# A hybrid decoder trunk on one core: who makes the low halves of four weight tiles of layer 0

## The chip, the cores and the metric

One of the eight cores of a Trainium2 chip runs the whole program. The metric is device time in microseconds (us) of one execution. The core has TensorE (PE in the profile, PEld for its weight loads), VectorE (DVE), ScalarE (ACT), GpSimd (POOL) and SyncE (SP); each runs its own instructions in order, and semaphores hold one back for another. TensorE multiplies into eight banks of PSUM; everything else lies in SBUF. Transfers (DMA) are issued by SP, by ScalarE and by GpSimd; only those of GpSimd add what they bring to what lies in SBUF.

## The reference, cut to what matters

Two layers of this, on 512 tokens of 1024 features, in float32:

```
h = rmsnorm(x) * (1 + sc1) + sh1                       # adaLN from c
u = h @ w_in                                           # 1024 x (256 + 3*256 + 3*512 + 3*1024)
u_pool, u_conv, b_conv, c_conv, q, k, v, gates = split(u)
y_pool = pool_mixer(u_pool)                            # trailing windows 2, 4, 8, 16
y_conv = b_conv * causal_short_conv(c_conv * u_conv)   # width 3
y_attn = moba_attention(rope(rmsnorm(q)), rope(rmsnorm(k)), v)   # blocks of 256
x += g1 * (sum_i sigmoid(gate_i) * (y_i @ p_i)) @ w_out
h2 = rmsnorm(x) * (1 + sc2) + sh2
x += g2 * ((silu(h2 @ w_gate) * (h2 @ w_up)) @ w_down)
```

The change touches four tiles of `w_in` in the first layer: the two that hold the lower half of the keys' rows, and the two column blocks (4 and 5) of `b_conv`, which gate the convolution.

## The kernel before, in words

**Layout.** Activations lie transposed, features on the 128 partitions and 512 tokens along the row. Weights come from HBM in one stream that the host has laid out in the order of use, as tiles of up to eight blocks of 128 by 128 (512 KB).

**Three products for one.** TensorE multiplies in a rounded form of float32 (`fp32r`). To keep float32's accuracy each operand is split into a high half, its rounded value, and a low half, what the rounding left. `mm3` adds three products, high by high, high by low and low by high. So each weight tile is fetched into a `raw` tile, its high half is copied into a `whi` tile by ScalarE, and its low half is made in a `wlo` tile, in one of two ways:

- `split_w` (lines 397 to 404): ScalarE copies the high half (line 399), VectorE subtracts it from the raw tile (line 402). Both read the raw tile.
- `split_by_transfer` (lines 416 to 424): ScalarE copies the high half (line 419) and then the negated high half into the `wlo` tile (line 421); then GpSimd issues a transfer that fetches the weights a second time and adds them to it (line 423). Only the first copy reads the raw tile.

There are three `raw` tiles and five each of `whi` and `wlo`. A `raw` tile is fetched anew by SP (line 239) when its last reader is through; a `whi` or `wlo` tile is written anew when TensorE has used it.

**Order.** The list `items` holds all weight tiles in the order of use. `load_w` loads the next one, `next_w` hands one out and keeps up to four loaded ahead. TensorE's instructions, and VectorE's that are marked with `pin`, keep the program's order; for the rest (ScalarE's copies, transfers) a planner sets the order on each engine at build time by its own estimate of when each can run. On the chip each engine then goes through its list in that order. Which buffer of a ring a tile gets follows from that order too.

**The stretch around the change, layer 0.** First come the queries and three column blocks (lines 987 to 1015), then three column tiles (6, 3 and 7). Then the keys and values, by `keys_values` (line 1043) with tiles from the class `KeyValue` (line 296): seven products of half-size matrices in place of eight, called forms, of 24 matmuls of 512 columns each, in the order B21, B11, R1, -V, B22, T3, T4. Each form uses two tiles, of 12 matmuls each. The first two forms (numbers 0 and 1 in `load`, line 322) take the keys' weights as they are, the others take sums that GpSimd's transfers build in two `w` tiles (`summed`, lines 313 to 315) and `big` tiles (`summed_rows`, lines 350 to 354). In layer 0 the first two forms are split by transfer, in layer 1 by VectorE (line 335). The raw tiles of the second form stay for VectorE's additions at line 338.

Behind the forms come single columns of eight blocks (`feature_tile`, 24 matmuls): gate columns 20, 28 and 21, then columns 4 and 5, each followed by a product of the pool mixer, then gate column 29 and the rest of the gates. `by_transfer` (line 426) decides which of them are split by transfer: those of the pool and attention projections and the columns above 20, so 28, 21 and 29 but not 20, 4 and 5. Meanwhile attention's pieces for the heads are dealt out among the matmuls. VectorE's last instruction of a piece of attention, line 872, hands its output to ScalarE and to TensorE's next matmuls.

Of the kernel before, what the change touches and what calls it, by code (L numbers as in the profile page):

```python
# [25 lines left out]
KT = D // P  # L26
# [15 lines left out]
C_BLOCKS = 8  # L42
# [41 lines left out]
def hybrid_trunk(ctx, tc, xT, ws, ada, cols, pool_w, qk_w, crow, pos, con, out):  # L84
# [12 lines left out]
    def nm(s):  # L97
        uid[0] += 1
        return f"{s}{uid[0]}"

    def bigt(dt=F32R):
        return big.tile([P, S], dt, tag="big", name=nm("big"))
# [10 lines left out]
    def w4(shape, dt=F32):  # L113
        return work.tile(shape, dt, tag="w4", name=nm("w4"), bufs=6)
# [42 lines left out]
    def pin(ins):  # L157
        return tc.keep_in_program_order(ins)
# [66 lines left out]
    def runs(l, blocks):  # L225

        i = 0
        while i < len(blocks):
            off, n, at = place[blocks[i]]
            j = i + 1  # L230
            while j < len(blocks) and place[blocks[j]] == (off, n, at + j - i):
                j += 1
            src = ws[l, off:off + n * P * P].rearrange("(p f) -> p f", p=P)
            yield i, j - i, src[:, at * P:(at + j - i) * P]
            i = j

    def fetch(tile, l, blocks):
        for i, n, src in runs(l, blocks):
            nc.sync.dma_start(tile[:, i:i + n].rearrange("p b n -> p (b n)"), src)
# [37 lines left out]
    class GateUp:  # L277
# [9 lines left out]
        def load(self, sub):  # L287
            if sub < 2:
                return self.pair[sub].first()
            if sub < 6:  # L290
                return self.pair[sub % 2].sums(sub // 2 - 1)
            raw = rawt()
            fetch(raw, self.l, self.pair[0].blocks(1, 1) + self.pair[1].blocks(1, 1))
            return split_w(raw, C_BLOCKS)

    class KeyValue:
# [25 lines left out]
        def load(self, sub):  # L322
            form, cp = divmod(sub, 2)
            if sub == 0:
                self.near, self.far = [None] * 2, [None] * 2
            if sub == 2:
                self.x = [w4([P, C_BLOCKS, P]) for _ in range(2)]
                for i in range(2):
                    self.summed(self.x[i], (1, 1), i)
            if form < 2:  # L330
                kk = 1 - form
                raw = self.raw(kk, 0, cp)
                if form == 1:
                    self.near[cp] = raw
                return split_by_transfer(raw, self.l, self.blocks(kk, 0, cp)) if self.l == 0 else split_w(raw, C_BLOCKS)
            if form in (2, 3):
                w = split_w(self.x[cp], C_BLOCKS)
                pin(V.tensor_add(self.x[cp], self.x[cp], self.near[cp]))
                if form == 2:
                    self.near[cp] = self.raw(1, 0, cp)  # L340
                    self.far[cp] = [bigt(F32) for _ in range(2)]
                    self.summed_rows(self.far[cp], (0, 0), cp)
                return w
            if form == 4:
                return split_w(self.x[cp], C_BLOCKS)
            if form == 5:
                return split_rows(self.far[cp])
            return split_w(self.raw(1, 1, cp), C_BLOCKS)
# [26 lines left out]
    for l in range(L):  # L375
# [7 lines left out]
        for blocks in first_part + list(feed_forward()):  # L383
            if not isinstance(blocks, list):
                if isinstance(blocks, int):
                    blocks = GateUp(l, blocks)
# [7 lines left out]
    def rawt():  # L394
        return wp.tile([P, C_BLOCKS, P], F32, tag="raw", name=nm("raw"), bufs=RAW)

    def split_w(raw, n):
        hi = wp.tile([P, C_BLOCKS, P], F32R, tag="whi", name=nm("whi"), bufs=5)
        A.activation(hi[:, :n], raw[:, :n], AF.Copy)  # L399
        lo = wp.tile([P, C_BLOCKS, P], F32R, tag="wlo", name=nm("wlo"), bufs=5)  # L400
        with tc.issue_after(hold[0].ins) if hold[0] is not None else nullcontext():
            ins = V.tensor_sub(lo[:, :n], raw[:, :n], f32(hi)[:, :n])  # L402
        pin(ins)
        return hi, lo


    def split_rows(tiles):
        hi = wp.tile([P, C_BLOCKS, P], F32R, tag="whi", name=nm("whi"), bufs=5)
        lo = wp.tile([P, C_BLOCKS, P], F32R, tag="wlo", name=nm("wlo"), bufs=5)
        rows = lambda t, i: t[:, 4 * i:4 * i + 4].rearrange("p b n -> p (b n)")  # L410
        for i, tile in enumerate(tiles):
            A.activation(rows(hi, i), tile, AF.Copy)
            pin(V.tensor_sub(rows(lo, i), tile, f32(rows(hi, i))))
        return hi, lo

    def split_by_transfer(raw, l, blocks):
        n = len(blocks)
        hi = wp.tile([P, C_BLOCKS, P], F32R, tag="whi", name=nm("whi"), bufs=5)
        A.activation(hi[:, :n], raw[:, :n], AF.Copy)  # L419
        lo = wp.tile([P, C_BLOCKS, P], F32R, tag="wlo", name=nm("wlo"), bufs=5)  # L420
        A.activation(lo[:, :n], f32(hi)[:, :n], AF.Copy, scale=-1.0)  # L421
        for i, m, src in runs(l, blocks):
            nc.gpsimd.dma_start(lo[:, i:i + m].rearrange("p b n -> p (b n)"), src, accum_op=ALU.add)  # L423
        return hi, lo

    def by_transfer(blocks):
        return blocks[0][0] in ("pool", "attn") or blocks[0][0] == "in" and blocks[0][2] > 20 and len(blocks) == KT

    split_after, last_hi = [None], [None]
# [3 lines left out]
    def load_w():  # L433
        while at[1] < min(at[0] + 1 + SUMS_AHEAD, len(items)):
            sums, sub = items[at[1]]
            if sums is not None and sub == 0:
                sums.begin()
            at[1] += 1
        sums, what = items[at[0]]
        at[0] += 1  # L440
        if sums is not None:
            return sums.load(what)
        l, blocks = what
        raw = rawt()
        with tc.issue_after(fetch_after[0].ins) if fetch_after[0] is not None else nullcontext():
            fetch(raw, l, blocks)
        if by_transfer(blocks):
            return split_by_transfer(raw, l, blocks)
        with tc.issue_after(split_after[0].ins) if split_after[0] is not None else nullcontext():
            return split_w(raw, len(blocks))  # L450
# [3 lines left out]
    def next_w(ahead=None):  # L454
        ahead = ahead_now[0] if ahead is None else ahead
        while at[0] < len(items) and len(loaded) <= ahead:
            loaded.append(load_w())
        return loaded.popleft()
# [97 lines left out]
    def ada_tasks(l, parts, early=False):  # L556
        every = [(part, j) for part in parts for j in range(KT)]
        kept, out = [], []
        load = lambda n: ada_load(l, *every[n], early, kept)

        def step(n):
            if early and n + 1 < len(every):
                load(n + 1)
            if not early:
                load(n)
            ada_step(l, *every[n], kept)

        if early:
            out.append((1.2, lambda: load(0)))
        for n, (part, j) in enumerate(every):  # L570
            out.append((1.2, lambda n=n: step(n)))
            if j == KT - 1:
                out.append((0.2, lambda part=part: ada_end(l, part)))
        return out
# [133 lines left out]
    def second(nrm, l, i, bank):  # L708

        hold[0] = None  # L710
        nrm.stat(BLOCK, S, bank)
        for k, lo, hi in HALVES[3:]:
            nrm.apply(l, i, k, lo, hi)

        loaded.append(load_w())
        for k, lo, hi in REST:
            nrm.apply(l, i, k, lo, hi)
# [240 lines left out]
    norm.first_hi(0)  # L958
    fetch_after[0] = step[4]
    loaded.append(load_w())  # L960
    split_after[0] = last_hi[0]
    norm.first_lo(0)
# [651 lines left out]
```

## Time and profile before

| | |
|---|---|
| median of 3 runs | 1435.55 us (1434.87 to 1435.87) |
| the profiled execution | 1438.11 us |
| its span, first to last instruction | 1436.3 us |
| granted clock of TensorE over the span | 0.998 |
| weight tiles split by transfer (line 423) | 66, 861 ns to issue one |
| weight tiles split by VectorE (line 402), fetched or summed | 170 and 84, 1181 and 1220 ns each |
| transfers of GpSimd (queue 0) | 80.76 MB, 27.8% of 16 engines' span |
| transfers of SP (queue 1) | 177.37 MB, 35.5% of 16 engines' span |

How to read it. The span is cut into what each engine does. A row of a timeline gives the start and the duration in us, engine, line, operation, what it writes and reads, and in brackets how long the engine was idle before and who ended that. A row of the waits gives the engine, what waited, who ended the wait, and then the total in us, the number of times and the longest. The chain is the work that ended last, followed back from the end: each piece is what the next one waited for. All times are in us from the start of the span. `whi` and `wlo` are the high and low halves of weights, `big` those of activations, `mm` and `pair` banks of PSUM; matmuls into `mm` with `wlo` second (`mm<-big,wlo`) are columns, those into `pair` with `wlo` first are forms.

### The profile page before, as it was taken

Reading aid. Unit: us, or ns where it says so; the run is one execution under the profiler, and the core shown is the slowest. Engines: PE = TensorE matmul, PEld = TensorE weight load, DVE = VectorE, ACT = ScalarE, POOL = GpSimd, SP = SyncE. Lnnn points to the kernel's source line nnn. Section 1 sums busy time; section 2 is a strip of 40 time slices with the busy share of each in tenths; the row PEclk is TensorE's granted clock in tenths of the full one; section 3 lists DMA queues with packets and bytes.
Section 4 is the critical chain, followed back from the end, with each engine's and each line's share of the span. In section 5 each row is a group of like instructions: output and inputs, shape, how many; then the busy total and the mean of one; then the engine's idle time right before and its main releaser. Section 6 shows DMA issues by size and latency. Waiting matters only on the chain.

```text
span 1436.3 us, 22185 instructions
## 1 busy us (share of the span) xinstructions
PE 1425.6 (99%) x8308; PEld 1256.1 (87%) x8308; DVE 1045.0 (73%) x1978; ACT 765.1 (53%) x1275; POOL 179.5 (12%) x246
## 2 busy tenths in 40 slices
PE   9999999999999999999999999999999999999999
PEld 8877887887989998989998888888889989999997
DVE  7889767649886867667788986665778747657663
ACT  5767667743554452535455676667336525425450
POOL 0111101110200210211001111111020103111200
PEclk9999999999999999999999999999999999999999
DMA  9878668897636766746527676667872537636522
GB/s 349 232 200 213 149 168 199 199 320 243 172 122 212 205 177 205 191 125 212 199 78 248 171 196 141 159 158 187 300 213 85 138 109 186 175 107 179 138 86 85
DMA packets 96587, 259.67 MB, mean 181 GB/s; under 512 B 12248, under 2 KB 24928, under 8 KB 96480
## 3 DMA queue, kind: packets, MB, share of 16 engines
q1 hardware_dynamic: 67312, 177.37, 35.5%
q0 software_dynamic: 28576, 80.76, 27.8%
q8 instruction: 65, 1.06, 0.3%
q14 instruction: 42, 0.34, 0.1%
q10 hardware_dynamic: 592, 0.14, 0.0%
HBM read 256.12 MB, written 2.10 MB: 180 GB/s over the span
## 4 chain that ended last, share of the span: by engine, by line
PE 89%; DVE 4%; DMA 4%; ACT 2%; issue 1%; SPq 0%; DVEq 0%; ACTq 0%; POOLq 0%
PE mm L155 77%; PE pair L155 11%; DMA raw<-in_ws 2%; PE mm L161 2%; DMA wlo<-in_ws 1%; DVE w L479 1%; DVE wlo L402 1%; DMA x<-in_xT 0%; DVE tmp L683 0%; DVE big L690 0%; ACT whi L419 0%; ACT wlo L421 0%; DVE big L702 0%; DVE big L1252 0%; ACT big L701 0%
## 5 line engine op out<-in xcount | busy, mean ns | idle before, releaser
L155 PE MATMUL mm<-big,whi 128*128 128x512 f32 (+1 forms) x4334 | 1073.4, 339 | 0.8 <-ACT big L701 0.6
L155 PEld LDWEIGHTS mm<-big,whi 128*128 128x128 f32 x4334 | 741.3, 190 | 87.2 <-issue 2.2
L155 PE MATMUL mm<-big,wlo 128*128 128x512 f32 (+1 forms) x2167 | 732.1, 338 | 1.1 <-DMA wlo<-in_ws 1.1
L155 PEld LDWEIGHTS mm<-big,wlo 128*128 128x128 f32 x2167 | 411.0, 190 | 46.0 <-ACT whi L419 1.5
L399 ACT ACTIVATE whi<-raw 128x1024 fp32r<-128x1024 f32 (+2 forms) x170 | 174.3, 1028 | 159.1 <-PE mm L155 92.5
L402 DVE TENSOR_TENSOR wlo<-raw,whi 128x1024 fp32r<-128x1024 f32 (+2 forms) x170 | 199.2, 1181 | 41.7 <-ACT whi L399 41.2
L399 ACT ACTIVATE whi<-w 128x1024 fp32r<-128x1024 f32 x84 | 88.8, 1058 | 154.6 <-PE mm L155 87.1
L402 DVE TENSOR_TENSOR wlo<-w,whi 128x1024 fp32r<-128x1024 f32 x84 | 101.1, 1220 | 29.1 <-ACT whi L399 28.4
L479 DVE SCALAR_TENSOR_TENSOR w<-w,csil 128x1024 f32<-128x1024 f32 x88 | 105.1, 1219 | 13.2 <-DMA w<-in_ada 13.2
L1301 DVE SCALAR_TENSOR_TENSOR x<-mm,mod,x 128x512 f32<-128x512 f32 (+1 forms) x89 | 61.5, 693 | 70.2 <-PE mm L155 69.9
L423 POOL DMA_DIRECT2D wlo<-in_ws x66 | 56.9, 861 | 401.4 <-ACT wlo L421 321.7
L261 POOL DMA_DIRECT2D w<-in_ws x72 | 47.1, 666 | 453.6 <-DVE wlo L402 210.9
L419 ACT ACTIVATE whi<-raw 128x1024 fp32r<-128x1024 f32 x66 | 70.0, 1061 | 50.8 <-PE mm L155 29.5
L155 PE MATMUL pair<-whi,big 128*128 128x512 f32 x256 | 83.0, 389 | 0.0
L263 POOL DMA_DIRECT2D w<-in_ws x72 | 64.4, 915 | 138.0 <-DMA w<-in_ws 131.8
L155 PE MATMUL pair<-big,whi 128*128 128x256 f32 (+1 forms) x392 | 78.9, 298 | 0.0
L421 ACT ACTIVATE wlo<-whi 128x1024 fp32r<-128x1024 f32 x66 | 69.3, 1054 | 0.6
L155 PEld LDWEIGHTS pair<-big,whi 128*128 128x128 f32 x392 | 63.4, 191 | 2.8
L155 PE MATMUL pair<-big,wlo 128*128 128x256 f32 (+1 forms) x196 | 58.4, 298 | 0.0
L155 PEld LDWEIGHTS pair<-whi,big 128*128 128x128 f32 x256 | 48.1, 188 | 9.9
L701 ACT ACTIVATE big<-big 128x512 fp32r<-128x512 f32 x52 | 32.4, 626 | 38.6 <-DVE big L1294 18.2
L155 PE MATMUL pair<-wlo,big 128*128 128x512 f32 x128 | 50.0, 390 | 1.4 <-DMA wlo<-in_ws 1.4
(239 smaller groups left out, 1411.7 us busy)
## 6 DMA issues: line engine op xcount, KB each, us to landing
raw<-in_ws SPq DMA_DIRECT2D x146, 512.0 KB, 4.3
w<-in_ada SPq DMA_DIRECT2D x88, 512.0 KB, 5.7
w<-in_ws POOLq DMA_DIRECT2D x144, 256.0 KB, 4.5
wlo<-in_ws POOLq DMA_DIRECT2D x66, 512.0 KB, 6.5
raw<-in_ws SPq DMA_DIRECT2D x64, 256.0 KB, 3.8
raw<-in_ws SPq DMA_DIRECT2D x24, 384.0 KB, 3.5
raw<-in_ws SPq DMA_DIRECT2D x16, 448.0 KB, 5.3
raw<-in_ws SPq DMA_DIRECT2D x36, 128.0 KB, 2.9
```

What stands on the lines that cost most here:

```text
L155: tc.keep_in_program_order(T.matmul(*a, **k))
L161: tc.keep_in_program_order(T.transpose(*a))
L261: nc.gpsimd.dma_start(dst, self.source(0, 1))
L263: nc.gpsimd.dma_start(dst, self.source(*other), accum_op=ALU.add)
L399: A.activation(hi[:, :n], raw[:, :n], AF.Copy)
L402: ins = V.tensor_sub(lo[:, :n], raw[:, :n], f32(hi)[:, :n])
L419: A.activation(hi[:, :n], raw[:, :n], AF.Copy)
L421: A.activation(lo[:, :n], f32(hi)[:, :n], AF.Copy, scale=-1.0)
L423: nc.gpsimd.dma_start(lo[:, i:i + m].rearrange("p b n -> p (b n)"), src, accum_op=ALU.add)
L479: return V.scalar_tensor_tensor(aw, aw, 1.0, csil, op0=ALU.mult, op1=ALU.mult, accum_out=mod[l][:, part, j:j + 1])
L701: A.activation(hi, src, AF.Copy)
L1301: V.scalar_tensor_tensor(x[k][:, lo:hi], src, mod[l][:, part, k:k + 1], x[k][:, lo:hi], op0=ALU.mult, op1=ALU.add)
```

## The change

In layer 0 the first form of keys and values (number 0, B21) makes its two low halves with VectorE, as layer 1 does, and columns 4 and 5 make theirs with ScalarE's negating copy and an adding transfer. Layer 1 and all other tiles are as before. `by_transfer` gets the layer as an argument.

```diff
@@ -332,7 +332,7 @@
                 raw = self.raw(kk, 0, cp)
                 if form == 1:
                     self.near[cp] = raw
-                return split_by_transfer(raw, self.l, self.blocks(kk, 0, cp)) if self.l == 0 else split_w(raw, C_BLOCKS)
+                return split_by_transfer(raw, self.l, self.blocks(kk, 0, cp)) if self.l == 0 and form else split_w(raw, C_BLOCKS)
             if form in (2, 3):
@@ -423,7 +423,9 @@
-    def by_transfer(blocks):
+    def by_transfer(blocks, l):
+        if l == 0 and len(blocks) == KT and blocks[0] in (("in", 0, 4), ("in", 0, 5)):
+            return True
         return blocks[0][0] in ("pool", "attn") or blocks[0][0] == "in" and blocks[0][2] > 20 and len(blocks) == KT
@@ -444,7 +446,7 @@
-        if by_transfer(blocks):
+        if by_transfer(blocks, l):
             return split_by_transfer(raw, l, blocks)
```

## The prediction, made before the changed kernel was run

> **What bounds the kernel now.** I read the page's first part, then TensorE's waits over the whole run, then the chain that ended last around the stretch that the change touches. The page:
>
> ```profile
> span 1436.3 us, 22185 instructions
> ...
> PE 1425.6 (99%) x8308; PEld 1256.1 (87%) x8308; DVE 1045.0 (73%) x1978; ACT 765.1 (53%) x1275; POOL 179.5 (12%) x246
> ```
>
> TensorE (PE) is busy for 99% of the span; 1436.3 - 1425.6 = 10.7 us is all that it idles. The change adds and removes no matmul, so it can gain only from those 10.7 us. TensorE's waits, from the longest on:
>
> ```profile
> PE pair L155 <- DMA wlo<-in_ws: 1.4, 1, 1.4
> PE mm L155 <- DVE tmp L872: 1.4, 1, 1.4
> ...
> PE mm L155 <- DMA wlo<-in_ws: 1.1, 1, 1.1
> ```
>
> Two of them wait for a low half (wlo) that a transfer adds to. Where they lie, from the chain of 50 to 125 us, and from TensorE's timeline, with the first low half of column 4 in a fence of its own, for later:
>
> ```profile
> 68.34 11.61 DMA wlo<-in_ws
> ...
> 85.58 5.44 PE mm L155 x24
> ...
> 112.36 7.25 DMA wlo<-in_ws
> ```
>
> ```profile
> 80.08 0.47 PE L155 MATMUL pair<-wlo,big 128*128 128x512 f32 x1 [1.42 <-DMA wlo<-in_ws]
> ...
> 119.74 0.47 PE L155 MATMUL mm<-big,wlo 128*128 128x512 f32 x1 [1.07 <-DMA wlo<-in_ws]
> ```
>
> ```profile
> 131.65 0.40 PE L155 MATMUL mm<-big,wlo 128*128 128x512 f32 x1
> ```
>
> 24 matmuls take 5.44 us, 0.227 each, while a record lasts 0.39 and so hides 0.16 of each gap. The stalls cost 1.42 + 0.16 = **1.58 us** at 80.08 (second form, first pair of row blocks) and 1.07 + 0.16 = **1.23 us** at 119.74 (column 28). Without its own stall the matmul at 80.08 comes at 80.08 - 1.58 = 78.50, and the one at 119.74 at 118.51. Each is the second matmul of its form or column, so the second form begins at 78.27, the first form 5.44 earlier at 72.83, and column 20, ahead of 28, at 118.28 - 5.44 = 112.84, where the keys' and values' last form is through.
>
> **Part one: the first form's low halves by VectorE.** ScalarE, GpSimd and VectorE before the first stall, each from its timeline, and one of VectorE's subtractions, which has the shape of the two that are added:
>
> ```profile
> 63.49 1.99 ACT L421 ACTIVATE wlo<-whi 128x1024 fp32r<-128x1024 f32 x2
> 65.39 0.61 ACT L701 ACTIVATE big<-tmp 128x512 fp32r<-128x512 f32 x1
> 65.91 1.04 ACT L419 ACTIVATE whi<-raw 128x1024 fp32r<-128x1024 f32 x1
> 66.99 1.06 ACT L421 ACTIVATE wlo<-whi 128x1024 fp32r<-128x1024 f32 x1
> ```
>
> ```profile
> 64.84 1.79 POOL L423 DMA_DIRECT2D wlo<-in_ws  x2 [11.64 <-ACT wlo L421]
> 66.31 1.20 POOL L315 DMA_DIRECT2D w<-in_ws  x1
> 68.34 0.86 POOL L423 DMA_DIRECT2D wlo<-in_ws  x1 [0.83 <-DVE big L1035]
> 71.33 0.86 POOL L423 DMA_DIRECT2D wlo<-in_ws  x1 [2.14 <-ACT wlo L421]
> ```
>
> ```profile
> 63.09 0.17 DVE L1142 TENSOR_TENSOR tmp<-tmp,big 128x16 f32<-128x16 f32 x1
> 66.04 0.69 DVE L702 TENSOR_TENSOR big<-tmp,big 128x512 fp32r<-128x512 f32 x1 [2.77 <-ACT big L701]
> ```
>
> ```profile
> 118.95 1.21 DVE L402 TENSOR_TENSOR wlo<-raw,whi 128x1024 fp32r<-128x1024 f32 x1
> ```
>
> Landing times (the last column, us), from DMA views cut to one issue each: the adding transfers of 64.84 and 71.33, and SP's raw load of 62, the second form's second:
>
> ```profile
> wlo<-in_ws POOLq DMA_DIRECT2D x1, 512.0 KB, 7.7
> ```
>
> ```profile
> wlo<-in_ws POOLq DMA_DIRECT2D x1, 512.0 KB, 11.2
> ```
>
> ```profile
> raw<-in_ws SPq DMA_DIRECT2D x1, 512.0 KB, 4.3
> ```
>
> Removed: two negating copies (the 1.99 us at 63.49) and the two adding transfers at 64.84. The chain's first stall hangs on both. The second form's first transfer is issued at 68.34, 0.29 us after its copy ends (66.99 + 1.06 = 68.05), and that copy stands behind the 1.99 us. Without them the issue is at about 68.34 - 1.99 = 66.35. Its landing falls too. Five transfers pass GpSimd's queue here (64.84 twice, 66.31, 68.34, 71.33); the first lands at 64.84 + 7.7 = 72.5, the fifth at 71.33 + 11.2 = 82.5, so they follow each other at (82.5 - 72.5) / 4 = 2.5 us. Two fewer in front are 5.0 us: 79.95 - 5.0 = 75 us against the 78.50 at which it is wanted. The bounds: with the 7.7 of a transfer that leads the queue it lands at 74.1, with all of today's 11.61 at 78.0, still in time. So I take the whole **-1.58 us**.
>
> Added: two subtractions of 1.21 us on VectorE (row 118.95). VectorE idles 2.77 us ahead of 66.04, between 63.26 and 66.04, and that wait itself ends with ScalarE's L701 at 65.39, which stands behind the removed copies. 2.42 us of work meet 2.77 us of idle time, and the first form's matmuls begin at 72.83, seven microseconds later. Cost: 0. If the gap closed, the queue behind would be the pool mixer's subtraction at 66.04 and the sums' input tiles, wanted at 85.58 at the earliest.
>
> What moves: the raw buffer of the first form is now held until VectorE has read it (64.5 at the latest, 63.26 + 1.21) where ScalarE's copy freed it at about 62. There are three such buffers, and SP fetches in order, so the second form's second load starts up to 2.5 us later. With its 4.3 it lands at 64.5 + 4.3 = 68.8, and ScalarE reads it at about 68.9 today (the issue at 71.33, less 0.29, less two copies of 1.06): nothing lost. Its transfer, which lands at 82.5, must now land by 78.50 + 2.72 = 81.2 (12 matmuls on); with the queue 5 us shorter it does, with all of today's 11.2 it is 1.3 late. So this part's bounds are -1.58 and -0.3.
>
> **Part two: columns 4 and 5 by ScalarE and transfers.**
>
> ```profile
> 97.28 0.63 ACT L412 ACTIVATE whi<-big 128x512 fp32r<-128x512 f32 x1 [1.04 <-DMA big<-in_ws]
> ...
> 111.02 1.99 ACT L421 ACTIVATE wlo<-whi 128x1024 fp32r<-128x1024 f32 x2
> ...
> 113.53 1.99 ACT L399 ACTIVATE whi<-raw 128x1024 fp32r<-128x1024 f32 x2
> 118.03 1.06 ACT L419 ACTIVATE whi<-raw 128x1024 fp32r<-128x1024 f32 x1 [2.51 <-DVE w L761]
> ...
> 127.25 1.05 ACT L421 ACTIVATE wlo<-whi 128x1024 fp32r<-128x1024 f32 x1
> ```
>
> ScalarE gains two copies of 1.05 us, 2.1 in all, behind the high halves at 113.53; it idles 2.51 us ahead of 118.03, so they are hidden: 0. (Without that cover they'd delay 118.03, column 29's high half, whose own copy waits to 127.25 anyway.) VectorE loses two subtractions of 1.21 (column 4's at 118.95 and column 5's behind it); TensorE waits for nothing of VectorE's there, so that is 0 too. The new transfers go out at about 113.53 + 1.99 + 2.1 = 117.6 and come behind those of 28 and 21 in the queue. How long they take, from the view of the wlo tiles, first at 60 to 145 us, then at 146 to 222, where fewer transfers meet:
>
> ```profile
> DMA to landing us min/median/max: 6.8/9.0/11.6
> ```
>
> ```profile
> DMA to landing us min/median/max: 5.0/5.2/7.9
> ```
>
> 117.6 + 11.6 = 129.2 in the worst case, against column 4's first use of a low half at 131.65 (130.07 once 1.58 us are gained): no stall, with 0.9 us to spare, 3.5 by the median of 9.0.
>
> The second stall, column 28's, moves with the first. Its transfer (112.36) stands behind ScalarE's queue, whose pace in this stretch is set by TensorE's forms, so both the landing and the want come 1.58 us earlier and the 1.23 stay. Two things push at it. For: the 1.04 us that ScalarE waits at 97.28 ends with a transfer of the same GpSimd queue that is 5 us shorter, and the fourth form's copies, the raw buffers that they free and the fetch of 28 all stand behind it; up to 1.0 earlier. Against: raw buffers of columns 4 and 5 are freed by ScalarE and not by VectorE at 118.95 + 1.21 = 120.2, so the next fetch, 512 KB, comes at about 114.6, into the flight of 28's transfer. That flight lasts 7.25 us now; by the rows above it is 5.0 at best and 9.0 in company, so at most 9.0 - 7.25 = +1.8. I take half of that difference, +0.9, for the one raw load that comes to it, and the whole lead, -1.0: **-0.1 us**, bounds -1.23 (the stall can't be less than none) and +1.8.
>
> The Trainium skill speaks against the change here: DMA: Bandwidth & Descriptors, "Issuing engines are not separate DMA queues", says that the transfers of all issuing engines run on the same 16 DMA engines and interleave. The two rows above agree (median 9.0 in company, 5.2 out of it). By that rule alone the added load costs and nothing is given back, and this term would be +0.9 in place of -0.1, the sum -0.7.
>
> Sum against the profiled execution: 1438.11 (span 1436.3 and 1.8 around it) - 1.58 - 0.1 = 1436.4. That execution lies 2.56 above the median of the three timed runs, 1435.55; I take the same difference off that: 1435.55 - 1.7 = **1433.9 us**. A measurement of this kernel can tell about 0.2%, 2.9 us, from no change, so the likeliest result is a small gain that counts as none: bounds -2.81 and +1.5, own range 1432.7 to 1437.0.
>
> **The rivals.**
>
> Both stalls go, and more with them. If 28's fetch gains its 1.0 and its flight doesn't lengthen, -2.81; the wait for VectorE's L872 (row 1.4, and 0.16 hidden) depends on raw loads and ScalarE's order behind them, which shift as buffers free earlier. If that goes too, -4.4: 1431.2. For it: three raw buffers set much of this stretch's order. Against: the work in front of L872 is attention's and the gates', which the change doesn't edit.
>
> Given back in full: 28's transfer meets two raw loads and takes 9.0, and the 1.0 of lead doesn't come. Then -1.58 + 1.8 = +0.2: 1435.8, no change. For it: the rule above; against: GpSimd's queue alone is freed by 5 us.
>
> Slower: column 4's added copy gets the wrong buffer. The order on ScalarE, and with it which of five low-half buffers a column gets, is not the program's but a planner's at build time. Column 29 shows the price: its high half is made at 118.03, its negating copy at 127.25, since its low half goes where column 28's lies until TensorE is through with 28 (118.28 + 1.23 + 5.44 = 124.95). If column 4 gets that place in the ring, its copy comes at 127.25 - 1.58 = 125.7, its transfer starts at 127.0 and with 9.0 lands at 136.0 where 130.07 is wanted: a stall of 5.9, and -1.7 + 5.9 = +4.2: 1439.8. It decides from an issue of column 4's transfer after 125.7 on (landing 134.7, a stall of 4.6, a loss over 2.9). For: two more writers of low halves move between engines, which can turn the ring. Against: counted back by five from column 4, the place is one of the last form's, free at 112.84.
>
> **How the numbers follow.** The small gain 0.55, given back 0.17 (both within 0.2%); both stalls and more 0.18 (faster); the wrong buffer 0.10 (slower). Faster 0.18, same 0.72, slower 0.10. The range reaches from the rival with three stalls gone, 1431.2, to 1437.2, the upper end of the likeliest case's bounds (+1.5) and 0.2 of the runs' spread, and leaves out the wrong buffer and about half of the first rival, whose losses of stalls may go further: about 0.2.
>
> **What would show it.** Right: TensorE has no wait for wlo in the second form; the second form's transfer is issued near 66.4 and lands before 78; two subtractions of 1.2 us stand in VectorE's gap at 63 to 66; the wait at column 28 is 0 to 2 us long and ends near 118; L421 for columns 4 and 5 by 118, no wait when their matmuls begin. Wrong: a wait at column 4 or 5, a wait for VectorE ahead of the first form at 72.8, or a copy of theirs beyond 124.

## The result, and the profile after

The changed kernel takes 1445.17 us (median of 6 runs, 1441.58 to 1450.01), the kernel before beside it 1436.64 (6 runs, 1434.87 to 1437.72). The ratio is 1.0065, 95% interval 1.0049 to 1.0081: **slower by 0.65%** (8.5 us between the medians), where a gain of 1.7 was forecast with 1437.2 as the upper end. The profiled execution of after is the fastest of its six, 1441.58, so its trace shows 3.47 us of the loss (1441.58 - 1438.11) and not all of it. Behind line 428 the lines of after are two higher than those of before (the waits and copies named L1214 and L1222 there are L1216 and L1224 here).

The page of after, and TensorE's waits from the longest on:

```profile
span 1439.5 us, 22178 instructions
...
PE 1428.2 (99%) x8308; PEld 1258.0 (87%) x8308; DVE 1045.1 (73%) x1978; ACT 766.4 (53%) x1275; POOL 180.0 (13%) x246
```

```profile
PE mm L155 <- ACT big L1216: 2.1, 1, 2.1
PE mm L155 <- ACT big L1224: 1.7, 1, 1.7
PE pair L155 <- POOL ones L207: 1.1, 1, 1.1
PE mm L155 <- DVE wlo L402: 0.7, 1, 0.7
```

Neither of the waits for a wlo that a transfer fills is named any more, and the 1.4 for L872 is gone from the head of the list. Three others stand in their place. TensorE's timeline says where, and that one is the old one under another name:

```profile
111.48 0.50 PE L155 MATMUL mm<-big,wlo 128*128 128x512 f32 x1 [0.68 <-DVE wlo L402]
...
119.37 0.47 PE L155 MATMUL mm<-big,wlo 128*128 128x512 f32 x1 [2.11 <-ACT big L1216]
...
120.67 1.05 PE L155 MATMUL mm<-big,whi 128*128 128x512 f32 x2
121.52 0.63 PE L155 MATMUL mm<-big,wlo 128*128 128x512 f32 x1
...
134.23 0.73 PE L155 MATMUL mm<-big,whi 128*128 128x512 f32 x2 [1.66 <-ACT big L1224]
```

With the 0.16 us that a record hides: 0.84 at column 20, which had no wait; 2.27 at column 28, which had 1.23; and 1.88 (with 0.22 hidden) at column 4's first matmul, which waits for a PSUM bank that ScalarE's tanh of a gate (L1224) has to empty. The row of 119.37 names ScalarE's L1216, the event nearest in time, whose output this matmul doesn't read; it is a wait for column 28's low half: the transfer issued at 111.36, below, lands 7.87 us later, at 119.23. From 120.24 on the rows change: three matmuls take 1.28 us (1.05 + 0.63 less the overlaps, from 120.67 to 121.95) and not 0.68. TensorE's clock is at half, as the busy time by stretches shows (the column before the last two is the granted clock, then the DMA engines' share, which comes out a little above 1 when they are full):

```profile
core 0: us, PE busy (x) PEld busy (x) DVE busy (x) ACT busy (x) POOL busy (x), PEclk, DMA share, GB/s
...
117.00:119.40 2.40, 0.29 (x3) 0.06 (x1) 2.40 (x8) 2.37 (x5) 0.34 (x1) 1.00 1.06 258
...
120.20:123.60 3.40, 3.40 (x10) 2.65 (x9) 3.21 (x8) 3.37 (x5) 0.00 (x0) 0.53 1.05 271
123.60:127.00 3.40, 3.40 (x17) 2.81 (x16) 0.39 (x1) 1.12 (x2) 0.00 (x0) 1.00 1.07 254
```

10 matmuls in 3.40 us where the next 3.40 us hold 17: seven pitches of 0.43 in place of 0.227, 1.4 us. So the wait of 2.27 costs 3.7. The balance of this execution: before 1.58 + 1.23 + 1.66 = 4.5; after 0.84 + 2.27 + 1.4 + 1.88 + 1.0 (small waits at 140 us) + 0.3 (what is left of L872) = 7.7, together +3.2 of the 3.47. The other five runs of after left no trace. Their mean clocks are 0.996, 0.995, 0.995, 0.993 and 0.996, in the profiled one 0.996; 98 runs of before in the comparisons below have 0.9975 on average. One stretch of 3.4 us at half clock takes 0.5 x 3.4 / 1440 = 0.0012 off the mean, so 0.9952 is about two such stretches more than before, some 3 us of the 8.5 (an estimate from these rows).

What VectorE, ScalarE and GpSimd did, from their timelines of after:

```profile
63.58 1.23 DVE L402 TENSOR_TENSOR wlo<-raw,whi 128x1024 fp32r<-128x1024 f32 x1 [1.82 <-ACT whi L399]
...
66.42 0.17 DVE L1144 TENSOR_TENSOR tmp<-tmp,big 128x16 f32<-128x16 f32 x1
67.30 0.69 DVE L704 TENSOR_TENSOR big<-tmp,big 128x512 fp32r<-128x512 f32 x1 [0.70 <-ACT big L703]
...
109.70 0.42 DVE L1217 SCALAR_TENSOR_TENSOR big<-tmp,big 128x256 fp32r<-128x256 f32 x1
...
110.20 1.22 DVE L402 TENSOR_TENSOR wlo<-raw,whi 128x1024 fp32r<-128x1024 f32 x1
```

```profile
62.49 1.06 ACT L399 ACTIVATE whi<-raw 128x1024 fp32r<-128x1024 f32 x1 [2.83 <-DMA raw<-in_ws]
...
110.03 2.94 ACT L421 ACTIVATE wlo<-whi 128x1024 fp32r<-128x1024 f32 x3
...
132.33 0.42 ACT L1119 ACTIVATE pwh<-tmp 128x256 fp32r<-128x256 f32 x1 [5.24 <-DMA tmp<-in_pool_w]
132.65 1.04 ACT L421 ACTIVATE wlo<-whi 128x1024 fp32r<-128x1024 f32 x1
133.60 0.58 ACT L1224 ACTIVATE big<-mm 128x512 f32<-128x512 f32 x1
```

```profile
66.31 0.86 POOL L423 DMA_DIRECT2D wlo<-in_ws  x1 [12.11 <-ACT wlo L421]
...
111.36 2.76 POOL L423 DMA_DIRECT2D wlo<-in_ws  x3 [31.71 <-ACT wlo L421]
115.31 0.86 POOL L423 DMA_DIRECT2D wlo<-in_ws  x1 [1.19 <-ACT wlo L421]
```

Read them against those of before. VectorE's second added subtraction (63.58) waits for ScalarE's high half, and that for the raw tile's load; the pool mixer's work, done by 63.26 before, now stands behind it, and its subtraction runs at 67.30 where it ran at 66.04. Column 20's subtraction (110.20) stands behind four operations for the values (L1217, the last at 109.70), which before came after it. It starts 1.24 us earlier than in before, but TensorE comes to column 20 2.44 us earlier (110.18 against 112.62); 0.74 of that it had before the first form began (72.10 against 72.84). ScalarE makes the negated copies of 28, 21 and 4 in one go (110.03), behind the high halves of all three. And it waits 5.24 us for the pool mixer's weights with the tanh behind it. The subtraction and its first reader in before, where it ended at 112.66, 0.4 us ahead of the matmul:

```profile
111.44 1.22 DVE L402 TENSOR_TENSOR wlo<-raw,whi 128x1024 fp32r<-128x1024 f32 x1
```

```profile
113.07 0.39 PE L155 MATMUL mm<-big,wlo 128*128 128x512 f32 x1
```

The transfers' landing times in 105 to 117 us, as the view of the wlo tiles gives them for after:

```profile
DMA to landing us min/median/max: 7.9/12.0/14.0
```

### The profile page after: what moved, and what is told of

Read it like the earlier page. It is cut to its first block, busy times and chain, and to the rows that moved or that the text cites. A ratio compares the mean times of both kernels' runs of the same rounds, so it can differ in the third digit from the quotient of the medians.

```text
span 1439.5 us, 22178 instructions
## 1 busy us (share of the span) xinstructions
PE 1428.2 (99%) x8308; PEld 1258.0 (87%) x8308; DVE 1045.1 (73%) x1978; ACT 766.4 (53%) x1275; POOL 180.0 (13%) x246
## 3 DMA queue, kind: packets, MB, share of 16 engines
q8 instruction: 65, 1.06, 0.3%
## 4 chain that ended last, share of the span: by engine, by line
PE 95%; DVE 2%; DMA 1%; ACT 1%; SPq 0%; issue 0%; DVEq 0%; ACTq 0%
PE mm L155 81%; PE pair L155 12%; PE mm L161 2%; DMA tmp<-in_pool_w 1%; DVE wlo L402 0%; DMA x<-in_xT 0%; SPq L196 0%; ACT big L703 0%; DVE big L704 0%; DVE w L481 0%; DVE big L1296 0%; DVE big L1136 0%; DVE big L1254 0%; SPq L1116 0%; DVE big L1217 0%
```

## The experiments

The first theory, from the two traces: part one gains its 1.58 us; the two added transfers fill the DMA engines (share 1.06 above), and what else is in flight lands late (theory A). Rivals: ScalarE's two added copies cost the time (B); part one itself does (C). Each run (5 to 12 executions) stands against the kernel before on the same chip. e1 to e8, e9 to e12 and e13 to e16 ran on three chips, on which the kernel before took 1435.7 to 1436.2 us, so across these groups the ratios are what to compare. The table comes first, what each was for behind it.

| run | what differs from before | median us | ratio, 95% interval |
|---|---|---|---|
| e1 | part one | 1442.1 | 1.0041 (1.0026 to 1.0056) |
| e2 | part two | 1447.0 | 1.0070 (1.0053 to 1.0086) |
| e3 | part one, ScalarE's copies of part two, no transfers | 1441.4 | 1.0040 (1.0026 to 1.0055) |
| e4 | part one, the transfers of part two, VectorE's copies | 1444.9 | 1.0056 (1.0038 to 1.0074) |
| e5 | part one behind the pool mixer | 1440.1 | 1.0023 (1.0011 to 1.0036) |
| e6 | part one, column 20 ahead | 1437.2 | 1.0007 (0.9999 to 1.0016) |
| e7 | part two, pool weights early | 1446.1 | 1.0069 (1.0053 to 1.0085) |
| e8 | e5 and e6 together | 1437.9 | 1.0010 (1.0002 to 1.0019) |
| e9 | both parts, column 20 ahead | 1439.4 | 1.0023 (1.0014 to 1.0033) |
| e10 | column 20 ahead alone | 1437.4 | 1.0003 (0.9994 to 1.0013) |
| e11 | part two, column 20 ahead | 1436.3 | 0.9998 (0.9989 to 1.0008) |
| e12 | half of part one, column 20 ahead | 1435.6 | 0.9993 (0.9985 to 1.0002) |
| e13 | part one, the values' evacuations behind | 1440.5 | 1.0030 (1.0019 to 1.0041) |
| e14 | both parts, the values' evacuations behind | 1445.3 | 1.0065 (1.0048 to 1.0081) |
| e15 | e9, pool weights early | 1446.6 | 1.0071 (1.0055 to 1.0088) |
| e16 | half of part one, part two, column 20 ahead | 1435.3 | 0.9996 (0.9986 to 1.0006) |

**Each part alone, and part two cut in two.** e1 leaves out the two lines for columns 4 and 5; e2 leaves out `and form`. In e3 the columns' low halves are made so, and in e4 so:

```diff
+        A.activation(lo, f32(hi), AF.Copy, scale=-1.0)      # e3
+        pin(V.tensor_add(lo, raw, f32(lo)))
...
+        pin(V.tensor_scalar(lo, f32(hi), -1.0, None, op0=ALU.mult))      # e4
+        for i, m, src in runs(l, blocks):
+            nc.gpsimd.dma_start(lo[:, i:i + m].rearrange("p b n -> p (b n)"), src, accum_op=ALU.add)
```

e1: 

> Part one alone: the first form's low halves by VectorE, columns 4 and 5 as in the kernel before. Theory A (the added transfers of columns 4 and 5 fill the DMA engines, and what else is in flight lands late): the 1.58 us wait at 80 us is gone, 0.3 to 0.8 may come back at column 20; no half clock near 120 us, no wait at 134 us; 1434.2 to 1436.0 against 1436.6 for the kernel before. Rival B (ScalarE's two added copies cost the time): the same. Rival C (part one itself costs: TensorE gets to column 20 earlier than VectorE's and ScalarE's work behind the forms): slower than before, 1438 to 1443, with the half clock near 120 us.

e2: 

> Part two alone: columns 4 and 5 by ScalarE's negating copy and an adding transfer, the first form as in the kernel before. Theory A: the wait at column 28 is 2 us or more, the pool mixer's weights land 8 us or more after their issue, a wait of over 1 us at 134 us; 1441 to 1448, 4 to 11 above the kernel before. Rival B: the same time, but the waits end with ScalarE's copies and no transfer is late. Rival C: 1436 to 1438, as the kernel before.

e3: 

> Part one, and for columns 4 and 5 ScalarE's two copies each as in the changed kernel, but VectorE adds the raw tile to the negated copy in place of a transfer. ScalarE's work is that of the changed kernel, the transfers are those of part one alone. Theory A: within 1 us of part one alone (1434 to 1436). Rival B: near the changed kernel, 1441 to 1447.

e4: 

> Part one, and for columns 4 and 5 the two adding transfers of the changed kernel, but the negated copy that they add to is made by VectorE. ScalarE's work is that of part one alone, the transfers are those of the changed kernel. Theory A: near the changed kernel, 1440 to 1448, with transfers of 9 us and more between 111 and 132 us and the pool mixer's weights late. Rival B: within 1 us of part one alone (1434 to 1436).

ScalarE's copies cost nothing (e3 1441.4, e1 1442.1): B falls. The transfers may cost something (e4 2.8 us over e1, with intervals that overlap). But part one alone loses 5.9 us where theory A had it gain 1.6, so A is not the whole, and part two alone loses as much as both parts together (1.0070 and 1.0065, the intervals overlap). e1's TensorE and VectorE:

```profile
96.01 0.50 PE L155 MATMUL mm<-wlo,big 128*128 128x512 f32 x1 [0.87 <-DVE wlo L402]
114.88 0.50 PE L155 MATMUL mm<-big,wlo 128*128 128x512 f32 x1 [1.98 <-DVE wlo L402]
123.44 0.47 PE L155 MATMUL mm<-big,wlo 128*128 128x512 f32 x1 [1.18 <-DMA wlo<-in_ws]
136.01 0.73 PE L155 MATMUL mm<-big,whi 128*128 128x512 f32 x2 [0.96 <-ACT big L1222]
```

```profile
62.27 1.23 DVE L402 TENSOR_TENSOR wlo<-raw,whi 128x1024 fp32r<-128x1024 f32 x1 [1.24 <-ACT whi L399]
66.21 1.22 DVE L402 TENSOR_TENSOR wlo<-raw,whi 128x1024 fp32r<-128x1024 f32 x1 [2.72 <-ACT whi L399]
...
69.94 0.69 DVE L702 TENSOR_TENSOR big<-tmp,big 128x512 fp32r<-128x512 f32 x1 [0.70 <-ACT big L701]
...
113.10 0.42 DVE L1215 SCALAR_TENSOR_TENSOR big<-tmp,big 128x256 fp32r<-128x256 f32 x1
...
113.60 1.22 DVE L402 TENSOR_TENSOR wlo<-raw,whi 128x1024 fp32r<-128x1024 f32 x1
```

Here VectorE waits 1.24 and 2.72 us for the first form's tiles inside its queue, and the mixer's subtraction is 3.9 us late (69.94 against 66.04). Column 20's subtraction is 2.2 late (113.60 against 111.44) and TensorE waits 2.15 us for it, with 3.4 us at half clock behind. In e2 there is none of that, but ScalarE waits 9.74 us for the pool mixer's weights, with a gate's tanh behind it, and TensorE 4.1 and 1.8 us for PSUM banks:

```profile
131.24 0.42 ACT L1119 ACTIVATE pwh<-tmp 128x256 fp32r<-128x256 f32 x1 [9.74 <-DMA tmp<-in_pool_w]
```

```profile
133.62 1.12 PE L161 MATMUL mm<-ident,w 128*128 128x128 f32 x4 [3.97 <-ACT big L1224]
...
136.14 1.22 PE L155 MATMUL mm<-big,whi 128*128 128x512 f32 x2 [1.40 <-ACT big L1224]
```

**VectorE's order, and the pool weights.** e5 gives VectorE the two subtractions only when the mixer's work is in its queue; e6 works out the keys' scale (`then`, a chain of small operations) one weight tile later in layer 0, so that column 20's subtraction comes ahead of it; e8 does both; e7 moves the pool weights' load and split.

```diff
-            then()
-            for _ in form(a, "T3", False):
-                pass
+            if l:
+                then()
+            for cp in form(a, "T3", False):
+                if l == 0 and cp == 0:
+                    then()
...
+        bulk.append((0.4, pool_weights))
         pool_chain(0, f_ps[0])
...
-        bulk.append((0.4, pool_weights))
```

e5: 

> Part one alone, with the first form's two subtractions given to VectorE behind the pool mixer's work (the step that the first query of the program order follows) in place of ahead of it. Theory C1 (in part one alone VectorE waits 1.2 and 2.7 us for raw tiles inside its queue, and all work behind is 3.9 us late): VectorE does the mixer's subtraction at 66 to 67 us and not at 69.9, the waits of 1.15 and 0.36 us near 95 us go; if that lateness is also what column 20 waits for, 1434 to 1436. Theory C2 (column 20's low half waits behind four evacuations of the values that the planner now puts ahead of it): the wait of about 2 us at column 20 and the half clock behind it stay, 1439 to 1441.

e6: 

> Part one alone, with column 20's subtraction ahead of the chain of small operations for the keys' scale on VectorE (in layer 0 the scale is worked out one weight tile later). Theory C2: the wait at column 20 (2.15 us) and the half clock behind it (1.4 us) go; 1438 to 1439.5. Rival (28's transfer is next, it lands as late as in part one alone, at 123.3): the wait at column 28 grows by what column 20 gives back, from 1.34 to 3 to 5 us, and the time stays at 1441 to 1443. C1: the waits near 95 us stay either way.

e7: 

> Part two alone, with the pool mixer's second weights loaded and split about 70 us earlier, ahead of the pool mixer's first chain. Theory A (the added transfers make that small load late, and ScalarE's copy of it holds up the gates' tanh and the PSUM banks): the waits of 4.1 and 1.8 us at 133 to 136 us and the half clock behind them go; 1438 to 1442. If the pool weights are not it (the banks wait for something else on ScalarE): 1445 to 1448 as part two alone.

e8: 

> Part one alone with both changes of VectorE's order: the first form's subtractions behind the pool mixer's work, column 20's ahead of the chain for the keys' scale. C1 and C2 together: no wait near 95 us and none at column 20, TensorE reaches column 28 about 1.6 us earlier than in the kernel before; 1434 to 1437 if 28's transfer moves with it, 1438 to 1441 with a wait of 3 us or more at column 28 if it doesn't. If neither order is the cause: 1441 to 1443, as part one alone.

e6 brings back 4.9 of the 5.9 us (1442.1 to 1437.2), more than the 2.6 to 4.1 that were expected: the wait at column 20 goes, the half clock behind it, and the wait at column 28 too. VectorE and GpSimd in e6 show why:

```profile
103.61 1.22 DVE L402 TENSOR_TENSOR wlo<-raw,whi 128x1024 fp32r<-128x1024 f32 x1
```

```profile
105.86 0.85 POOL L423 DMA_DIRECT2D wlo<-in_ws  x1 [25.74 <-DVE rq L731]
109.14 0.86 POOL L423 DMA_DIRECT2D wlo<-in_ws  x1 [2.44 <-ACT wlo L421]
```

Column 20's subtraction is done at 104.8 and not 114.8, and with it the planner has put column 28's negated copy right behind its high half: its transfer goes out at 105.86, in e1 at 115.10. (The releaser in the first row is only the event nearest in time; ScalarE's copy ended at 105.56, and the issue follows such a copy by 0.29 us in before too.) e5 has the mixer back in time (65.70); the wait near 96 us goes and 2 us come back (the intervals overlap), but it keeps 2.28 at column 20, and 3.2 at column 28. So these two waits don't come from the mixer's lateness. e8 is no better than e6. The pool weights' early load changes nothing for part two (e7): the wait is then 3.46 us at column 28, with half clock behind it.

**Column 20 ahead in the kernel before, with part two, with both, with half of part one.** The half: `and form` becomes `and (form or cp)`, so only the first of the first form's two tiles is VectorE's.

e9: 

> The whole change, with column 20's subtraction ahead of the chain for the keys' scale on VectorE (as in the run of part one alone with that order, 1437.2). Theory A (the transfers of columns 4 and 5 cost by what they delay in the DMA engines, 2.8 us by the two runs with VectorE's and ScalarE's copies): 1439 to 1442, with landing times of 9 us and more behind 111 us and a wait for the pool mixer's weights or a gate's bank near 130 us. Rival (part two costs only where column 20's late subtraction has pushed the fetches of the columns together): 1436.5 to 1438.

e10: 

> The kernel before with column 20's subtraction ahead of the chain for the keys' scale, nothing else. If that order frees column 20's raw tile and with it the fetch and the transfer of column 28 (issued 6 us earlier in part one alone with this order), the wait of 1.23 us at column 28 goes: 1434 to 1435.5. If the chain for the keys' scale is then late for attention: 1436 to 1438.

e11: 

> Part two alone with column 20's subtraction ahead. Against the kernel before with the same order it prices the two columns' copies and transfers alone. Theory A: 3 us or more above it, 1438 to 1442. Rival (as above, the fetches pushed together): within 1 us of it.

e12: 

> Half of part one: the first of the first form's two tiles by VectorE, the second by transfer as in the kernel before, and column 20's subtraction ahead. Theory C1 (VectorE's wait for the second raw tile makes the pool mixer's and the sums' work late): the mixer's subtraction runs at 66 to 67 us, the wait of 1.58 us at 80 us is still gone or below 0.5; 1434 to 1436, below part one with this order (1437.2). If what is left there comes from ScalarE's order at the gates (a wait of 1.18 us at column 4): 1436.5 to 1437.5.

Part two with column 20 ahead costs nothing (e11 against e10: 0.9998 and 1.0003), where it cost 10 us without: the rival of e11 holds, theory A does not, though the same bytes move in the same stretch. In the kernel before the new order is worth nothing (e10). The whole change with it keeps 3.6 of its 8.5 us (e9); half of part one with it loses nothing (e12; the 1.6 us against e6 are within the two intervals).

**What part one still costs.** e13 and e14 put `pin` on L1215, which keeps the values' four evacuations behind column 20's subtraction, and edit nothing else; e15 and e16 ask what is left in e9.

e13: 

> Part one alone, with only the values' evacuations (four of VectorE's 0.42 us operations) kept behind column 20's subtraction, as the kernel before has them. Theory C2 (these four make column 20's low half late): the subtraction ends 1.8 us earlier, the wait at column 20 falls from 2.15 to about 0.4 us and the half clock behind it goes; 1438 to 1439.5 against 1442.1 of part one alone. Rival (what matters is that column 20's subtraction comes ahead of the scale's chain, so that the transfer of column 28 is issued 5 us earlier): the wait at column 28 takes over, 1440.5 to 1442.5.

e14: 

> The whole change with the same four evacuations kept behind column 20's subtraction. Column 20's wait (0.85 us) goes; column 28's (2.27) and the pool weights' (1.88) have other causes, the transfers and loads that go out together behind 111 us: 1443 to 1445.5 against 1445.2. If the evacuations are the cause of all of it: 1439 to 1441.

e15: 

> The whole change with column 20's subtraction ahead and the pool mixer's second weights loaded some 70 us earlier. With the first of these alone a wait of 2.77 us at 131 us was left, where the weights land at 129.2 to 129.9. If they are its cause it falls to the 1.18 us that part one alone has there: 1437 to 1438. If not (the transfers of columns 4 and 5 themselves, or ScalarE's order): 1439 to 1440.5.

e16: 

> The whole change but for the first form's second tile, which goes by transfer as before, with column 20's subtraction ahead. If VectorE's wait for the second raw tile is what makes part two cost 2 us on top of part one (1439.35 against 1437.2) where it cost nothing without part one (1436.25 against 1437.4): 1435 to 1437. If part two costs 2 us with any part one: 1437.5 to 1438.5.

The evacuations are a small part. In e13 the wait at column 20 falls to 1.23 and the half clock goes, but column 28 waits 1.8 us in its place, as the rival had it; for the whole change (e14) nothing is gained, with 5.2 us at column 28. So it is column 20's place ahead of the scale's chain, and the transfer of 28 that goes out with it, that decides. The two waits in e13:

```profile
112.49 0.50 PE L155 MATMUL mm<-big,wlo 128*128 128x512 f32 x1 [1.07 <-DVE wlo L402]
119.87 0.47 PE L155 MATMUL mm<-big,wlo 128*128 128x512 f32 x1 [1.64 <-DMA wlo<-in_ws]
```

e16 shows what is left: with the second tile of the first form back on a transfer, both parts of the change stand and the time is that of before (0.9996), 4.0 us below e9. What is left in e9 thus comes with VectorE's second tile. Its one long wait is at column 4, 2.77 us for a gate's PSUM bank (2.55 in the row below, and what the last record hides), where the pool weights land at 129.9 us and in e16 at 127.2. e15 was to show that those are its cause, and failed: without them in that place the planner puts the pool mixer's split ahead of the same tanh, ScalarE waits 2.6 us for VectorE there, and TensorE 4.2, and 4.2 again at the like place in layer 1, which got the early load too. So e9 and e16, which differ in that tile alone, show that it costs the 4 us; by which of the things that stand ahead of that tanh is open, since no run took one away without putting another there. e9's row:

```profile
130.91 0.74 PE L155 MATMUL mm<-big,whi 128*128 128x512 f32 x2 [2.55 <-ACT big L1226]
```

The two traces lead further back than the pool weights. These fly as long in both (7.7 us in the median in e9, 7.4 in e16), but are issued 2.3 us later in e9 (120.89 against 118.60). All of ScalarE's work from column 28's high half to that tanh is 2.3 to 2.7 us later in e9, and TensorE is not. The high half in e9, then in e16:

```profile
106.89 1.06 ACT L419 ACTIVATE whi<-raw 128x1024 fp32r<-128x1024 f32 x1 [2.20 <-DMA raw<-in_ws]
```

```profile
104.61 1.06 ACT L419 ACTIVATE whi<-raw 128x1024 fp32r<-128x1024 f32 x1 [0.60 <-DMA raw<-in_ws]
```

It waits for its raw tile, which SP fetched 0.69 us later (101.73 against 101.04) and which took 5.1 us where it took 3.5. That fetch took 3.2 us in before and after, 3.3 in e6 and 4.9 in e1, the last three with both tiles on VectorE, so the longer flight doesn't follow from the second tile alone, and its cause is open. The two profiled executions are only 1.0 us apart (1438.10 and 1437.06), so this wait is not the whole of the 4.0.

Busy time by stretches in e16, where the transfers of columns 4 and 5 go out at 113.98:

```profile
core 0: us, PE busy (x) PEld busy (x) DVE busy (x) ACT busy (x) POOL busy (x), PEclk, DMA share, GB/s
...
111.00:121.00 10.00, 10.00 (x46) 8.28 (x45) 10.00 (x29) 8.11 (x13) 2.11 (x4) 1.00 1.05 272
121.00:132.00 11.00, 11.00 (x54) 9.11 (x53) 8.03 (x22) 7.34 (x10) 1.71 (x2) 1.00 1.04 253
```

The DMA engines are as full as in after (1.05 and 1.04), and TensorE never stops: in this run full queues cost nothing, and column 28's transfer, which is wanted first, goes out at 107.05 where it goes out at 111.36 in after. No run beat the kernel before by more than its interval.

## Why the prediction was wrong, point by point

- **What bounds the kernel**: right. TensorE's idle time was the stake, and the two waits named were the ones that moved.
- **The gain of part one, -1.58**: right as far as it goes. The second form's transfer was issued at 66.31 (66.35 forecast), landed 5.2 us later at 71.5 (75, bounds 74.1 to 78), and the wait is gone. That it landed ahead of its bounds is luck: the planner had also moved a transfer of the sums (L315) from 66.31 to 53.32, out of its way, and the prediction didn't have that.
- **"2.42 us of work meet 2.77 us of idle time. Cost: 0"**: the step that failed in part one. Part one alone loses 5.9 us (e1), so what it gives back is 7.5 and not 0. The gap was not open to this work: the second subtraction waits for a raw tile that landed at 62.45 before, and 1.06 us of ScalarE, and its place in the queue is ahead of the mixer's work, which filled the time up to 63.26 before. So the cover that I had named was lost: the pool mixer's subtraction came 1.26 us late in after and 3.9 in e1. I put the price of that at nothing because the sums' input is wanted at 85.58; it shows in e1 as the wait at 96 us, which e5 takes away. The larger part is another: 4.9 of the 5.9 us come back when column 20's subtraction is put ahead (e6), and the waits at 114 and 123 us stay when only the mixer is in time again (e5). The second tile is worth 4.0 us in the whole change (e16 against e9); in part one alone it is worth 1.6 (e12 against e6), which is not clear of noise.
- **Column 20 has no term in the sum**: the prediction asks of columns 4 and 5 whether TensorE waits for VectorE there, rightly finds no wait, and doesn't ask it of column 20. In before column 20's subtraction (111.44) was only 0.4 us ahead of its want. In after TensorE came 2.44 us earlier and VectorE 1.24, and that is the wait of 0.84; in e1 the subtraction was 2.2 us late, and the wait 2.15.
- **Column 28, -0.1**: failed by its lead. The flight grew by 0.62 (7.25 to 7.87; I took +0.9). The want came 1.41 earlier. But the issue came only 1.0 earlier (112.36 to 111.36), where I had counted 1.58 for TensorE's pace and 1.0 for the lead on top: 1.41 - 1.00 + 0.62 = +1.03 and not -0.1. The bounds held it (+1.8); what they did not hold is the 1.4 us of half clock that a wait of 2.27 us brought and one of 1.23 did not.
- **Columns 4 and 5, no stall with 0.9 us to spare**: right for what I looked at, no wait for their low halves; and the copies hide (e3). What I did not list is who else has a load in that stretch: the pool weights, 2.3 to 3.7 us in flight before and 10 to 12 in after, with a pinned copy on ScalarE ahead of a gate's tanh.
- **The Trainium skill's rule that spoke against it** (DMA: Bandwidth & Descriptors, "Issuing engines are not separate DMA queues") agrees with after's share of 1.06 and its flights of 12.0 us in the median; e11 and e16 show nearly the same share (1.02 to 1.05) without a loss, so the rule alone does not price the change.
- **The order of the work**: I said that the order on ScalarE is the planner's, and used it for one rival (the wrong buffer for column 4, which did not happen: its transfer went out by 115). Everywhere else I took the order of before as given. It was not: the evacuations moved ahead of column 20, column 28's copy behind column 4's high half. By e1 to e6 and e2 to e11, putting one subtraction ahead on VectorE, with what the planner re-sorted behind it, is worth 4.9 and 10.8 us, most or all of what each part costs.
- **The chances**: slower had 0.10, by a mechanism that did not occur. One of the right ones, the mixer's lateness, was in the text as a cover ("if the gap closed, the queue behind would be ...") without a price; column 20's place was not in it. The wait for L872, which the rival with three stalls gone names, did shrink to 0.3 in this trace, and that didn't help.
- **A reading**: a column's low half is read by its third matmul, not its second, so column 20 began at 112.62 and not at 112.84. Nothing else hangs on it.

## What to carry to other kernels

Work moved onto an in-order engine costs what it and the work behind it wait for, not only what it takes: ask when its inputs land and what stands behind it, before fitting it into a gap. Where a planner sets the order, a local edit re-sorts everything behind; compare the two orders before comparing durations, and pin the one instruction whose place matters (here column 20's subtraction) before judging the edit. Check every wait that has less slack than the edit gains: the next one in line takes the gain.

## What the runs showed of the hardware that was not expected

TensorE's clock fell to half for about 3.4 us behind waits of 2.27 us (after), 2.15 (e1), 2.21 (e3) and 2.36 (e4), which cost some 1.4 us more each time. It did not behind waits of 2.28 (e5, at column 20) and 2.77 (e9), and did behind all the longer ones, from 3.2 us (e5, at column 28) to 5.2 (e14), for about 3.4 or 7 us. Of the single waits of 1.9 us and less none in before, after, e6, e8, e12, e13 and e16 was followed by it, but one of 1.89 (e10, at 219 us) and one of 1.77 (e2, at 227) were, for 3.4 us each. The Trainium skill, TensorE: Matmul & The Clock Gate, "Part 1: The HAM clock gate", has a free-running window of 3413 ns and half rate after an idle window of about 3.4 us. The length agrees with the stretches of 3.4 us here, and a free-running window fits that waits of the same length do and don't trip it; but waits of 1.77 and 2.15 us are well short of a whole idle window, and the measurement decides.
